# z's projection first, k tile by k tile, z loaded whole per head, and the first W_out weights split during the last merge

## The chip, the cores and the metric

The kernel runs on one core of one Trainium2 chip. The metric is device microseconds from start to end of one execution; lower is better. Engines are called TensorE (PE in the rows, PEld for its weight loads), VectorE (DVE), ScalarE (ACT), GpSimd (POOL) and SyncE (SP, whose queue issues all DMAs here).

## The reference

One layer of a streaming encoder block, 1024 positions of width 1024, all in float32:

```python
h = x @ w_in                                   # 1024 x 7688
(qa, ka, va, ub, qc, kc, vc, zc, bc, ac, gate_a, gate_b, gate_c) = split(h)
ya = chunked_rel_attention(qa, ka, va, rel_bias)          # 8 heads of 64
yb = conformer_conv(ub, ...)                              # GLU, 31 taps, LayerNorm, SiLU
yc = gated_deltanet(qc, kc, vc, zc, bc, ac, ...)          # 4 heads of 128, o * silu(z) at its end
mix = sum over b of sigmoid(gate_b) * (y_b @ w_branch[b])
x = LN1(alpha * x + mix @ w_out)
x = LN2(alpha * x + relu(x @ w_up)**2 @ w_down + sigmoid(x @ w_pg) * (p @ w_pp))
```

`zc` is the 512-column output gate of the third branch: z, used only at the end of `gated_deltanet`.

## The kernel before, in words

Every float32 product is made of three matmuls: each operand is split into a high part (a ScalarE copy to a rounded type) and a low part (the difference, `split_lo`, on VectorE or GpSimd), and high x high, high x low and low x high are summed in a PSUM bank. There are eight banks in three groups, `pj` (2), `fj` (2) and `m` (4) (L93). Most large SBUF tiles are 4 KB slots of one group of 30 (`slot`, L84 to L87), handed out in program order.

The code is a list of steps. A scheduler orders them by priority, which is the order in the program, except that steps inside `tc.high_priority(offset=-1000000)` (L752) come last: they are fillers, which each engine takes up when nothing else is ready. The result is one fixed order of instructions per engine; on SP, too, a DMA that waits holds up all behind it.

- L193 to L203: the transposed x is loaded as two halves of eight k tiles (16 DMAs of 256 KB, first half first), converted and split into `xs` (16 slots).
- `v_proj` (L219), `qk_proj` (L235): the attention's projections. `v_proj` for the first four heads reads weights of 264 columns and writes one `pj` bank per 128 positions. Then 32 steps of attention: `attn_scores` (L257, scores, softmax) and `attn_out` (L284).
- The fillers (L752 to L774): first `side_proj` (L703) for the four 128-column tiles of z, each 48 matmuls into the `fj` banks, copied out by ScalarE (L707) and stored to `z_d` in DRAM; then `side_glu` (L710) for four tiles of the convolution's input, 96 matmuls each (sigmoid tile, then the other), then the 24 tiles of the merge gates. The Conformer convolution (`b_conv`, L634, 30 multiply-adds on VectorE per tile and half, into `ca`) can run as soon as the first GLU tile is in DRAM, its LayerNorm (`b_norm`) behind it.
- DeltaNet: for each head `dn_proj` (L394), `dn_s1` (L419), the 32x32 block inverses (`dn_inv`, L509, 31 dependent pairs of VectorE operations on `X`), `dn_s2` (L532), `dn_scan` (L588, eight dependent steps), `dn_out` (L615). The loop at L795 to L799 starts head h+1's projection before head h's scan. `dn_out` loads z a half at a time into a tile `z` with one buffer (L622), takes Silu, multiplies and stores yc (L631).
- `merge` (L720) three times, for ya, yb and yc: `yload` loads a branch's output back (L689), converts and splits it; each of eight output tiles d is 24 matmuls in `pj` and `fj` banks; sigmoid of the stored gates, product and sum into `mix`. The last merge splits `mix[d]` into `mh`, `ml` (L738, L739).
- Then the pools of that part are closed. `out_cols` (L852) takes 256 columns of W_out at a time: four loads of 256 KB with `lload` (L826), ScalarE copies (L822) and GpSimd splits, then 24 matmuls of 256 columns for each of eight position tiles in an `m` bank. The per-layer input, up and down stages follow; the change does not touch them.

Of the kernel before, what the change touches and what calls it, by code (L numbers as in the profile page):

```python
# [9 lines left out]
F32 = mybir.dt.float32  # L10
F32R = mybir.dt.float32r
# [43 lines left out]
def hybrid_block(ctx, tc, x, xT, pT, w_in, relb, conv_w, conv_b, cln_g, cln_b, dnw, a_log, dt_bias,  # L55
# [10 lines left out]
    def phase(name, waits="pool"):  # L66

        if scoped[0] is not None:
            scoped[0].close()
        st = ExitStack()  # L70
        pool = st.enter_context(tc.tile_pool(name=name, bufs=1, reuse_waits=waits))
        scoped[0] = st

        def alloc(shape, dt, tag, bufs, name):
            return pool.tile(shape, dt, tag=tag, bufs=bufs, name=name)

        return alloc
# [8 lines left out]
    def slot(shape, dt=F32, name="g"):  # L86
        return gp.tile(shape, dt, tag="g", bufs=NSLOT, name=name)  # L87
# [27 lines left out]
    def split_lo(eng, lo, src, hi):  # L115
        eng.tensor_tensor(lo, src, hi.bitcast(F32), ALU.subtract)  # L116
# [23 lines left out]
    def wview(w, k0, kt, c0, cols):  # L140
        return w[k0 * P:(k0 + kt) * P, c0:c0 + cols].rearrange("(k p) c -> p k c", p=P)
# [49 lines left out]


    xs = [(slot([P, T], F32R, name=f"xh{k}"), slot([P, T], F32R, name=f"xl{k}")) for k in range(NK)]  # L193
    xr = []
    for hf in range(2):
        sl = slice(512 * hf, 512 * hf + 512)
        for k in range(NK):
            if hf == 0:
                xr.append(slot([P, T], name="xr"))
            raw = xr[k][:, sl]  # L200
            SY.dma_start(raw, xT[k * P:(k + 1) * P, sl])
            S.activation(xs[k][0][:, sl], raw, AF.Copy)
            split_lo(V, xs[k][1][:, sl], raw, xs[k][0][:, sl])  # L203

    ya_d = dr.tile([4, P, T], F32, name="ya_d")
    yb_d = dr.tile([4, P, T], F32, name="yb_d")
# [2 lines left out]
    gc_d = dr.tile([CH * NT, P], F32, name="gc_d")  # L209
    glu_d = dr.tile([4, P, T], F32, name="glu_d")  # L210
    cv_d = dr.tile([4, P, T], F32, name="cv_d")
    z_d = dr.tile([4, P, T], F32, name="z_d")
    sg_d = dr.tile([3, NK, P, T], F32, name="sg_d")


# [316 lines left out]
    def dn_s2(h, o):  # L532
# [52 lines left out]
        for hf in hfs:  # L585
            V.tensor_copy(ch3(o["W"])[:, hf * 4:hf * 4 + 4, :], pw[hf])

    def dn_scan(h, o):  # L588
        O = o["vb"]
        ss = mp.tile([P, 8], F32, tag="ss", bufs=4, name="ss")  # L590
        st = None
        for c in range(NT):
            cs = slice(c * P, (c + 1) * P)
            pb = bank("m", name="scan")
            pb2 = bank("m", name="scano")
            pk, pss, po = pb[:, 0:P], pb[:, P:2 * P], pb2[:, 0:P]
            vn = O[:, cs]
            if c > 0:
                PE.matmul(pk, lhsT=o["W"][:, cs], rhs=st, start=True, stop=True)
                V.tensor_tensor(vn, vn, pk, ALU.subtract)  # L600
                PE.matmul(po, lhsT=o["qg"][:, cs], rhs=st, start=True, stop=False)
            if c < NT - 1:
                PE.matmul(pss, lhsT=o["kdec"][:, cs], rhs=vn, start=True, stop=True)
                ns = mp.tile([P, P], F32, tag="S", bufs=2, name="S")
                if c == 0:
                    V.tensor_copy(ns, pss)
                else:
                    V.scalar_tensor_tensor(ns, st, vec["egl"][:, h, c:c + 1], pss, ALU.mult, ALU.add)
                st = ns
            PE.matmul(po, lhsT=o["aT"][:, cs], rhs=vn, start=(c == 0), stop=True)  # L610
            S.activation(vn, po, AF.Copy, scale=o["rq"][:, c:c + 1])
            S.activation(po, po, AF.Square, scale=o["rq"][:, c:c + 1], accum_out=ss[:, c:c + 1])
        return O, ss

    def dn_out(h, O, ss):  # L615
        V.tensor_scalar(ss, ss, 1.0 / P, RMS_EPS, ALU.mult, ALU.add)
        r = mp.tile([P, 8], F32, tag="ss", bufs=4, name="r")
        pow_mh(r, ss, 8)
        for hf in range(2):
            sl = slice(512 * hf, 512 * hf + 512)  # L620
            c8 = slice(4 * hf, 4 * hf + 4)
            z = dn([P, 512], F32, "z", 1, "z")  # L622
            SY.dma_start(z, z_d[h][:, sl])
            S.activation(z, z, AF.Silu)
            V.tensor_tensor(ch3(O)[:, c8, :], ch3(O)[:, c8, :], bc_last(r[:, c8], P), ALU.mult)
            tp = bank("m", name="to")
            for c4 in range(4):
                c = hf * 4 + c4
                PE.transpose(tp[:, c4 * P:(c4 + 1) * P], O[:, c * P:(c + 1) * P], ident)
            V.scalar_tensor_tensor(O[:, sl], tp, ng_s[:, 0:1], z, ALU.mult, ALU.mult)  # L630
            SY.dma_start(yc_d[h][:, sl], O[:, sl])  # L631
# [71 lines left out]
    def side_proj(off, func, dst, name):  # L703

        for _, sl, r in side_mm(off, name):
            t = fs([P, 512], F32, "fs", 3, "fs")
            S.activation(t, r, func)  # L707
            SY.dma_start(dst[:, sl], t)

    def side_glu(i):  # L710
# [5 lines left out]
        for h, sl, r in side_mm(O_UB + P * i, f"fa{i}"):  # L716
            V.tensor_tensor(sg[h], r, sg[h], ALU.mult)
            SY.dma_start(glu_d[i][:, sl], sg[h])

    def merge(b, dram, first, last):  # L720
        ys = yload(dram)
        for d in range(NK):
            wb = [wload(wview(w_branch[b], 0, 4, P * d, P), 4, P, f"wbr{b}{d}")]
            if first:
                mix[d] = slot([P, T], name=f"mix{d}")
            for hf, sl, py in mm_b(ys, wb, tag=("pj", "fj"), name="pbr"):
                sg = fs([P, 512], F32, "fs", 3, "sgl")
                SY.dma_start(sg, sg_d[b, d][:, sl])
                S.activation(sg, sg, AF.Sigmoid)
                if first:  # L730
                    V.tensor_tensor(mix[d][:, sl], py, sg, ALU.mult)
                else:
                    V.tensor_tensor(sg, py, sg, ALU.mult)
                    V.tensor_tensor(mix[d][:, sl], mix[d][:, sl], sg, ALU.add)
            if last:
                mh = slot([P, T], F32R, name=f"mh{d}")
                ml = slot([P, T], F32R, name=f"ml{d}")
                S.activation(mh, mix[d], AF.Copy)  # L738
                split_lo(V, ml, mix[d], mh)  # L739
                mixs[d] = (mh, ml)  # L740
# [7 lines left out]
    def cp(shape, dt, tag, bufs, name):  # L748
        return fpool.tile(shape, dt, tag=tag, bufs=bufs, name=name)

    at = phase("at")
    with tc.high_priority(offset=-1000000):  # L752
        for h in range(CH):
            side_proj(O_ZC + P * h, AF.Copy, z_d[h], f"fz{h}")
        adt = cst.tile([P, 8], F32, name="adt")
        SY.dma_start(adt[:, 0:4], rows_bcast(a_log, 4))
        SY.dma_start(adt[:, 4:8], rows_bcast(dt_bias, 4))
        dnw_s = cload(dnw, [P, 12, KC], "dnw_s")
        cw_s = cload(conv_w, [P, 4, KB], "cw_s")
        cb_s = cload(conv_b, [P, 4], "cb_s")  # L760
        cg_s = cload(cln_g, [P, 4], "cg_s")
        cbb_s = cload(cln_b, [P, 4], "cbb_s")
        ng_s = cload(norm_g.rearrange("a (p o) -> p (a o)", o=1), [P, 1], "ng_s")
        for i in range(4):
            side_glu(i)
        for n, (b, d) in enumerate([(b, d) for b in range(3) for d in range(NK)]):
            side_proj(O_GATE[b] + P * d, AF.Copy, sg_d[b, d], f"fg{b}{d}")
            if n in (8, 12):
                for i in range(4):
                    b_conv(i, 0 if n == 8 else 1)  # L770
            if n in range(12, 12 + 4 * 1, 1):
                b_norm((n - 12) // 1)
            if n in range(17, 17 + 4 * 1, 1):
                b_norm(4 + (n - 17) // 1)  # L774
# [11 lines left out]
        return dn_s1(h, dn_proj(h))  # L786

    def dn_b(h, o):
        dn_s2(h, o)
        dn_out(h, *dn_scan(h, o))  # L790

    st = [None] * CH
    st[0] = dn_a(0)
# [32 lines left out]
    def lload(src, kt, cols, name):  # L826
        raw = lraw(name + "r")
        v = raw.rearrange("p (k c) -> p k c", k=kt)
        SY.dma_start(v, src)
        hi, lo = hilo(raw, name, G)  # L830
        return hi.rearrange("p (k c) -> p k c", k=kt), lo.rearrange("p (k c) -> p k c", k=kt)
# [19 lines left out]

    def out_cols(q):  # L852
        c0 = 256 * q
        ws = [lload(wview(w_out, k0, 2, c0, 256), 2, 256, f"wo{q}{k0}") for k0 in range(0, NK, 2)]
        for t in range(NT):
            xr = eo([P, 256], F32, "xres", 4, "xres")
            SY.dma_start(xr, xv[:, t, c0:c0 + 256])
            po = bank("m", name="pout")[:, :256]
            mm_a(Acc(po, 24), mixs, ws, slice(t * P, t * P + P))
            V.scalar_tensor_tensor(x1[t][:, c0:c0 + 256], xr, ALPHA, po, ALU.mult, ALU.add)  # L860
            V.bn_stats(lst[t][:, q, :], x1[t][:, c0:c0 + 256])
            if q == 3:
                ln1_t(t)
# [434 lines left out]
```

## Time and profile before

| | |
|---|---|
| runs | 1966.6, 1966.61, 1970.63 us, median 1966.61 |
| profiled execution | 1967.85 us, of which the span from first to last instruction is 1965.8 |
| instructions | 25832, of them 9265 matmuls |
| TensorE busy | 95% of the span |
| VectorE, ScalarE, GpSimd busy | 64%, 43%, 23% |
| mean granted TensorE clock | 0.979 |
| DMA | 244.66 MB, 124 GB/s on average |

A matmul counts as busy from its start to its modelled end, and consecutive ones overlap, so pitch (start to start) and counts tell more of TensorE than busy time. Idle time of an engine that is not the bottleneck costs nothing. PEclk is the granted TensorE clock as a share of 2.4 GHz.

### The profile page before, as it was taken

What the parts mean: (1) busy time and instruction counts of PE and PEld (TensorE: products, weight loads), DVE (VectorE), ACT (ScalarE), POOL (GpSimd) and SP (SyncE); (2) the same over time, 40 slices, a digit from 0 to 9 for tenths busy, and PEclk for the clock granted to TensorE, in tenths of its full rate; (3) what the DMA queues carried; (4) which work ended last, traced back from release to release, by engine and by line L of the source; (5) the groups of instructions that cost most, each with busy time, mean ns of one, the idle gap of its engine ahead of it and who ended that gap; (6) DMA issues with size and microseconds to landing.
All of it is one profiled execution on the core that took longest, in us unless ns stands there. A gap on an engine that the chain in (4) does not pass through costs nothing. (4 is left out here: it accounts for less than half of the span.)

```text
span 1965.8 us, 25832 instructions
## 1 busy us (share of the span) xinstructions
PE 1858.8 (95%) x9265; PEld 1553.0 (79%) x9265; DVE 1252.4 (64%) x2193; ACT 848.1 (43%) x1534; POOL 460.1 (23%) x385
## 2 busy tenths in 40 slices
PE   7999999999999989999999999989999999999996
PEld 6889887787777868777877898768888877778775
DVE  3343499799997747673376348764433326875978
ACT  4544545553332343433454216545555544333333
POOL 3323323343323122222120233223222310000001
PEclk9999999999999999999999999999999999999998
DMA  6212222133423233243453535763332357652542
GB/s 187 55 52 77 66 65 65 50 92 91 135 67 99 74 91 102 74 136 90 148 186 116 178 109 177 252 209 128 108 119 96 125 218 240 219 167 95 184 145 90
DMA packets 211471, 244.66 MB, mean 124 GB/s; under 512 B 23888, under 2 KB 130448, under 8 KB 211344
## 3 DMA queue, kind: packets, MB, share of 16 engines
q1 hardware_dynamic: 211344, 243.03, 39.0%
q8 instruction: 73, 1.20, 0.3%
q14 instruction: 54, 0.44, 0.1%
HBM read 183.17 MB, written 59.80 MB: 124 GB/s over the span
## 5 line engine op out<-in xcount | busy, mean ns | idle before, releaser
L646 DVE SCALAR_TENSOR_TENSOR ca<-ci,cw_s,ca 128x512 f32<-128x512 f32 x240 | 208.0, 867 | 3.2
L942 PE MATMUL pda<-bh,ah 128*128 128x512 f32 x256 | 97.6, 396 | 8.9 <-ACT bh L1160 7.8
L190 POOL TENSOR_TENSOR mv<-mv,nhalf 128x1 f32<-128x1 f32 x16 | 17.2, 1086 | 362.2 <-DVE mv L653 362.2
L943 PE MATMUL pda<-bl,ah 128*128 128x512 f32 x256 | 100.7, 393 | 0.0
L944 PE MATMUL pda<-bh,al 128*128 128x512 f32 x256 | 100.4, 393 | 0.0
L280 POOL TENSOR_SCALAR st<-st,mx 128x640 f32<-128x640 f32 (+2 forms) x64 | 51.4, 805 | 177.1 <-DVE mx L279 161.8
L942 PE MATMUL pdb<-bh,ah 128*128 128x512 f32 x192 | 74.8, 402 | 7.7 <-DVE x L1202 7.7
L1160 ACT ACTIVATE ah<-draw 128x1024 fp32r<-128x1024 f32 x32 | 33.9, 1060 | 102.8 <-PE pda L943 51.3
L1113 DVE TENSOR_TENSOR r<-puc,r 128x512 f32<-128x512 f32 x16 | 11.1, 692 | 103.3 <-PE puc L944 103.3
L943 PE MATMUL pdb<-bl,ah 128*128 128x512 f32 x192 | 76.4, 398 | 0.0
L944 PE MATMUL pdb<-bh,al 128*128 128x512 f32 x192 | 75.7, 397 | 0.0
L277 ACT ACTIVATE st<-st,mx 128x640 f32<-128x640 f32 (+2 forms) x64 | 44.5, 696 | 69.3 <-DVE mx L273 69.2
L942 PEld LDWEIGHTS pda<-bh,ah 128*128 128x128 f32 x256 | 48.6, 190 | 20.9 <-ACT bh L1160 9.0
L273 DVE CUSTOM_DVE_ANT_0 st<-sc,nb 128x320 f32<-128x320 f32 (+2 forms) x64 | 30.8, 485 | 45.9 <-PE sc L271 42.9
L944 PEld LDWEIGHTS pda<-bh,al 128*128 128x128 f32 x256 | 48.8, 190 | 10.3
L943 PEld LDWEIGHTS pda<-bl,ah 128*128 128x128 f32 x256 | 48.8, 191 | 10.2
L707 ACT ACTIVATE fs<-fj 128x512 f32<-128x512 f32 x56 | 33.0, 589 | 49.0 <-PE fj L164 30.7
L116 DVE TENSOR_TENSOR al<-draw,ah 128x1024 fp32r<-128x1024 f32 x32 | 39.1, 1221 | 23.0 <-ACT ah L1160 23.0
L307 ACT ACTIVATE ph<-tp 128x512 fp32r<-128x512 f32 (+2 forms) x72 | 36.6, 525 | 39.6 <-PE tp L303 31.3
L404 DVE SCALAR_TENSOR_TENSOR c<-pc,dnw_s,c 128x511 f32<-128x511 f32 (+2 forms) x72 | 52.5, 732 | 1.4 <-ACT c L402 1.2
L527 DVE TENSOR_TENSOR X<-X,tm 32x31 f32<-32x31 f32 (+15 forms) x124 | 50.9, 411 | 2.4
L116 DVE TENSOR_TENSOR pl<-tp,ph 128x512 fp32r<-128x512 f32 (+2 forms) x72 | 42.3, 595 | 14.9 <-ACT ph L307 14.3
(1589 smaller groups left out, 6276.5 us busy)
## 6 DMA issues: line engine op xcount, KB each, us to landing
draw<-h_d SPq DMA_DIRECT2D x48, 512.0 KB, 4.8
wu<-in_w_up_dram SPq DMA_DIRECT2D x32, 512.0 KB, 3.9
h_d<-r SPq DMA_DIRECT2D x64, 256.0 KB, 2.2
draw<-in_w_down_dram SPq DMA_DIRECT2D x32, 512.0 KB, 5.1
sg_d<-fs SPq DMA_DIRECT2D x48, 256.0 KB, 2.2
sgl<-sg_d SPq DMA_DIRECT2D x48, 256.0 KB, 3.0
wg<-in_w_pg_dram SPq DMA_DIRECT2D x36, 256.0 KB, 5.5
cb<-in_w_down_dram SPq DMA_DIRECT2D x16, 512.0 KB, 8.5
```

The lines of the kernel that those rows point to most:

```text
L116: eng.tensor_tensor(lo, src, hi.bitcast(F32), ALU.subtract)
L277: S.activation(st[:, :nk], st[:, :nk], AF.Exp, scale=-1.0, bias=mx[:, nm:nm + 1], accum_out=mx[:, 2:3])
L280: G.tensor_scalar(st[:, :nk], st[:, :nk], mx[:, 3:4], 1.0, ALU.mult, ALU.mult)
L307: S.activation(ph[:, :n], tp[:, :n], AF.Copy)
L404: V.scalar_tensor_tensor(acc[:, 512 * hf + s_:512 * hf + 512], pp[:, :512 - s_], cw[:, 3 - s_:4 - s_], acc[:, 512 * hf + s_:512 * hf + 512 ...
L527: V.tensor_tensor(X3[:, jj + 1:32, 0:ncol], X3[:, jj + 1:32, 0:ncol], tv, ALU.subtract)
L646: V.scalar_tensor_tensor(acc, t[:, H - s_:H - s_ + 512], cw_s[:, i, H - s_:KB - s_], acc, ALU.mult, ALU.add)
L707: S.activation(t, r, func)
L942: PE.matmul(out_, lhsT=ah, rhs=bh, start=first, stop=False, skip_group_check=True)
L943: PE.matmul(out_, lhsT=ah, rhs=bl, start=False, stop=False, skip_group_check=True)
L944: PE.matmul(out_, lhsT=al, rhs=bh, start=False, stop=last, skip_group_check=True)
L1160: S.activation(hi, src, AF.Copy)
```

## The change

z is computed before anything else: `z_start` reserves all eight banks (two halves of four tiles), loads x and z's weights k tile by k tile and adds each k tile's 24 matmuls as it arrives. ScalarE then copies the banks out to `z_d`. The splits of z's weights are VectorE's. The four `side_proj` calls for z are gone from the fillers. Before a head's `dn_s2`, `z_load` loads the whole z of the head into a slot and takes Silu once; `dn_out` reads halves of it. In the last merge, before `mix[4]` is split, `wo_first` loads the first 256 columns of W_out into slots, in two loads of 512 KB, and splits them on ScalarE and VectorE; `out_cols(0)` uses these.

```diff
-    xr = []
-    for hf in range(2):
-        sl = slice(512 * hf, 512 * hf + 512)
+    z_d = dr.tile([4, P, T], F32, name="z_d")
+
+    def z_start():
+        banks = {}
+        for i, tag in enumerate(("m", "m", "pj", "fj")):
+            for h in range(2):
+                banks[i, h] = bank(tag, name="pz")
+
+        def zmm(i, h, lhsT, rhs, first, last):
+            PE.matmul(banks[i, h], lhsT=lhsT, rhs=rhs, start=first, stop=last, skip_group_check=True)
+
         for k in range(NK):
-            if hf == 0:
-                xr.append(slot([P, T], name="xr"))
-            raw = xr[k][:, sl]
-            SY.dma_start(raw, xT[k * P:(k + 1) * P, sl])
-            S.activation(xs[k][0][:, sl], raw, AF.Copy)
-            split_lo(V, xs[k][1][:, sl], raw, xs[k][0][:, sl])
+            raw = slot([P, T], name="xr")
+            xh, xl = xs[k]
+            for h in range(2):
+                sl = slice(h * 512, h * 512 + 512)
+                SY.dma_start(raw[:, sl], xT[k * P:(k + 1) * P, sl])
+                if h == 0:
+                    wr = wp.tile([P, 528], F32, tag="wr", bufs=2, name=f"wz{k}r")[:, :512]
+                    SY.dma_start(wr, w_in[k * P:(k + 1) * P, O_ZC:O_ZC + 512])
+            wh = wp.tile([P, 528], F32R, tag="wh", bufs=6, name=f"wz{k}h")[:, :512]
+            wl = wp.tile([P, 528], F32R, tag="wl", bufs=6, name=f"wz{k}l")[:, :512]
+            S.activation(xh[:, 0:512], raw[:, 0:512], AF.Copy)
+            S.activation(wh, wr, AF.Copy)
+            split_lo(V, xl[:, 0:512], raw[:, 0:512], xh[:, 0:512])
+            split_lo(V, wl, wr, wh)
+            S.activation(xh[:, 512:], raw[:, 512:], AF.Copy)
+            split_lo(V, xl[:, 512:], raw[:, 512:], xh[:, 512:])
+            for h in range(2):
+                sl = slice(h * 512, h * 512 + 512)
+                for n, (w, xx) in enumerate(((wh, xh), (wh, xl), (wl, xh))):
+                    for i in range(4):
+                        zmm(i, h, w[:, i * P:(i + 1) * P], xx[:, sl], k == 0 and n == 0, k == NK - 1 and n == 2)
+        for h in range(2):
+            for i in range(4):
+                t = fs([P, 512], F32, "fs", 3, "fs")
+                S.activation(t, banks[i, h], AF.Copy)
+                SY.dma_start(z_d[i][:, h * 512:h * 512 + 512], t)
...
+    def z_load(h, o):
+        z = o["z"] = slot([P, T], name=f"z{h}")
+        SY.dma_start(z, z_d[h])
+        S.activation(z, z, AF.Silu)
+
...
-    def dn_out(h, O, ss):
+    def dn_out(h, o, O, ss):
...
-            z = dn([P, 512], F32, "z", 1, "z")
-            SY.dma_start(z, z_d[h][:, sl])
-            S.activation(z, z, AF.Silu)
+            z = o["z"][:, sl]
...
+    def wo_first():
+
+        for kk in range(2):
+            raw = slot([P, 4, 256], name=f"wo{kk}r")
+            hi, lo = slot([P, 4, 256], F32R, name=f"wo{kk}h"), slot([P, 4, 256], F32R, name=f"wo{kk}l")
+            SY.dma_start(raw, wview(w_out, 4 * kk, 4, 0, 256))
+            S.activation(hi, raw, AF.Copy)
+            split_lo(V, lo, raw, hi)
+            wo0.extend((hi[:, 2 * i:2 * i + 2, :], lo[:, 2 * i:2 * i + 2, :]) for i in range(2))
+
...
+            if last and d == 4:
+                wo_first()
             if last:
                 mh = slot([P, T], F32R, name=f"mh{d}")
...
+    z_start()
     at = phase("at")
     with tc.high_priority(offset=-1000000):
-        for h in range(CH):
-            side_proj(O_ZC + P * h, AF.Copy, z_d[h], f"fz{h}")
...
     def dn_b(h, o):
+        z_load(h, o)
         dn_s2(h, o)
-        dn_out(h, *dn_scan(h, o))
+        dn_out(h, o, *dn_scan(h, o))
...
-        ws = [lload(wview(w_out, k0, 2, c0, 256), 2, 256, f"wo{q}{k0}") for k0 in range(0, NK, 2)]
+        ws = wo0 if q == 0 else [lload(wview(w_out, k0, 2, c0, 256), 2, 256, f"wo{q}{k0}") for k0 in range(0, NK, 2)]
```

## Rows read from the trace of the kernel before

**Rows 1.** The page's busy time, share of the span and instructions of each engine.

```profile
PE 1858.8 (95%) x9265; PEld 1553.0 (79%) x9265; DVE 1252.4 (64%) x2193; ACT 848.1 (43%) x1534; POOL 460.1 (23%) x385
```

**Rows 2.** Stretches: length, busy us (count) of PE, PEld, DVE, ACT, POOL; PEclk, DMA share, GB/s.

```profile
0.00:57.00 57.00, 44.78 (x251) 38.86 (x252) 20.10 (x34) 22.14 (x40) 18.59 (x25) 0.97 0.53 162
83.00:236.50 153.50, 153.50 (x895) 135.02 (x895) 63.28 (x184) 78.18 (x163) 49.01 (x59) 1.00 0.23 64
236.50:502.00 265.50, 255.49 (x1293) 212.77 (x1292) 237.70 (x445) 131.90 (x265) 91.13 (x81) 0.98 0.26 74
502.00:631.00 129.00, 118.85 (x529) 95.81 (x528) 115.99 (x227) 39.15 (x86) 43.64 (x26) 0.96 0.35 97
1043.30:1060.00 16.70, 13.26 (x45) 10.01 (x45) 8.02 (x12) 6.76 (x9) 1.45 (x2) 0.80 0.26 93
1086.00:1100.00 14.00, 9.22 (x52) 8.60 (x51) 4.07 (x6) 4.40 (x7) 7.98 (x6) 0.76 0.79 250
1750.00:1800.00 50.00, 50.00 (x222) 41.39 (x222) 29.58 (x30) 19.57 (x20) 0.00 (x0) 1.00 0.25 81
```

**Rows 3.** The same for tiles pv, fj and pv alone: columns PE, PEld, DVE, ACT.

```profile
0.00:57.00 57.00, 29.20 (x192) 27.39 (x192) 3.39 (x14) 2.61 (x8) 0.97 0.53 162
...
0.00:57.00 57.00, 19.90 (x59) 12.62 (x60) 0.00 (x0) 1.19 (x2) 0.97 0.53 162
...
50.90:56.90 6.00, 6.00 (x48) 5.81 (x47) 0.50 (x2) 0.38 (x1) 1.00 0.00 0
```

**Rows 4.** Timeline of the start: start, us, engine, operation, count, idle before and releaser.

```profile
3.59 0.63 ACT L202 ACTIVATE xh<-xr 128x512 fp32r<-128x512 f32 x1 [1.51 <-DMA xr<-in_xT_dram]
...
4.61 0.63 ACT L202 ACTIVATE xh<-xr 128x512 fp32r<-128x512 f32 x1 [0.40 <-DMA xr<-in_xT_dram]
...
6.61 0.81 PE L164 MATMUL pv<-wv00h,xh 128*128 128x264 f32 x2 [6.61 <-ACT wv00h L133]
...
14.06 0.63 PE L164 MATMUL fj<-xl,fz0h 128*128 128x512 f32 x1
...
14.49 0.63 PE L164 MATMUL fj<-xh,fz0l 128*128 128x512 f32 x1
...
82.82 0.80 PE L269 MATMUL sc<-kh,q 128*128 128x128 f32 x4
```

**Rows 5.** The same for fj (PE, PEld, DVE, ACT), ca (DVE, ACT), X (DVE, POOL).

```profile
83.00:236.50 153.50, 54.56 (x220) 40.48 (x221) 0.68 (x1) 4.18 (x7) 1.00 0.23 64
...
236.50:370.00 133.50, 80.48 (x92) 0.00 (x0) 0.97 0.23 63
...
510.00:625.00 115.00, 27.01 (x63) 1.74 (x1) 0.96 0.35 98
...
864.00:899.00 35.00, 21.89 (x63) 1.26 (x1) 0.95 0.29 85
```

**Rows 6.** Timeline around the last head's output and the last merge's start.

```profile
1038.41 0.46 SPq L631 DMA_DIRECT2D yc_d<-c  x1
...
1043.38 0.32 SPq L689 DMA_DIRECT2D yr<-yc_d  x1
...
1045.92 0.75 DVE L630 SCALAR_TENSOR_TENSOR c<-to,ng_s,z 128x512 f32<-128x512 f32 x1 [9.18 <-ACT z L624]
...
1046.70 0.32 SPq L631 DMA_DIRECT2D yc_d<-c  x1
...
1046.90 0.79 PE L164 MATMUL pbr<-yh,wbr20h 128*128 128x512 f32 x1 [3.44 <-ACT yh L690]
...
1048.71 0.32 SPq L689 DMA_DIRECT2D yr<-yc_d  x1
```

**Rows 7.** Timeline around the first W_out matmul.

```profile
1089.82 1.23 DVE L116 TENSOR_TENSOR ml<-mix,mh 128x1024 fp32r<-128x1024 f32 x1 [1.18 <-ACT mh L738]
...
1090.36 1.12 PE L164 MATMUL pout<-wo00h,mh 128*128 128x256 f32 x4 [4.03 <-ACT wo00h L822]
```

**Rows 8.** Timeline of TensorE in the down stage.

```profile
1703.12 1.07 PE L942 MATMUL pda<-bh,ah 128*128 128x512 f32 x4
```

More of the change, by code (lines that the diff above doesn't have):

```diff
@@ L211, in hybrid_block @@
     cv_d = dr.tile([4, P, T], F32, name="cv_d")
-    z_d = dr.tile([4, P, T], F32, name="z_d")
     sg_d = dr.tile([3, NK, P, T], F32, name="sg_d")
@@ L718, in side_glu @@
             SY.dma_start(glu_d[i][:, sl], sg[h])
+    wo0 = []
+    def wo_first():
[6 more added lines that the diff above has]
+            wo0.extend((hi[:, 2 * i:2 * i + 2, :], lo[:, 2 * i:2 * i + 2, :]) for i in range(2))
     def merge(b, dram, first, last):
```

## Prediction

> **What bounds the kernel now.** The page comes first: TensorE is busy for 95% of the span and no other engine for more than 64% [rows 1], so time goes only where TensorE stands or runs at half clock. The table by stretches says where that is [rows 2]. Full speed is taken from the down stage: 222 matmuls of 512 columns in 50.0 us at clock 1.00, a pitch of 0.225 us. A 264-column one takes 6.00 / 48 = 0.125 us [rows 3]; a 256-column one I put at half of 0.225, 0.113 us. Three of the stretches are what the change aims at:
> - 0 to 57 us holds 192 matmuls of v_proj and 59 fillers of z [rows 3]: 192 x 0.125 + 59 x 0.225 = 37.3 us of work, so 19.7 us are lost. The first matmul starts at 6.61 us, and at 14 us two matmuls still stand 0.43 us apart, the 1.2 GHz level [rows 4].
> - 1043.3 to 1060 us holds 45 matmuls, 10.1 us of work: 6.6 us lost, 3.4 of them in one wait for the last head of yc [rows 6], the rest at half clock behind it (0.80 over 16.7 us is 6.7 us at half).
> - 1086 to 1100 us holds 52 matmuls, nearly all of W_out: 5.9 us of work, 8.1 lost. TensorE waits 4.03 us for the first W_out weights [rows 7] and then runs some 6.7 us at half clock (0.76 of 14).
>
> From 83 to 236.5 us TensorE is never idle. From 236.5 to 631 VectorE is the full engine, 90% busy in both stretches [rows 2]. TensorE's instructions stand in one fixed order, so a stretch of it without waits can't get shorter by moving work within it; only a loss can go.
>
> **Start.** z's 192 matmuls are not new: they leave the filler queue and come first. The second transfer of the program is converted at 4.61 us [rows 4]; in the changed order that place is held by z's first weights, so the first matmul can go at 4.61 + 0.63 = 5.2 us. Each k tile brings three transfers of 256 KB. At the 162 GB/s that the first 57 us average [rows 2] the 786 KB take 4.9 us; ScalarE needs 3 x 0.63 us, VectorE three splits of 512 columns, where one of 1024 takes 1.23 [rows 7]. The 24 matmuls of a k tile take 5.4 us at full clock and 10.3 at half, so loads and conversions lie under them; without that cover the eight k tiles would go at the feed's pace, 8 x 4.9 = 39 us, which is still less than the 43.2 of the matmuls. The weight loads wait for one of two raw buffers, and behind each on SP stands the next x load; with 5.4 us of matmuls per turn that wait is covered too. The clock: from the two later stretches I take 6.7 us at half, which loses 3.3; upper end 9.3 us (5.2 to the slow pair at 14.5 [rows 4]), 4.6 lost. Handing the banks over: the third of eight ScalarE copies frees v_proj's first bank, 1.9 us, while half 1 still has 12 matmuls, 2.7 us. Between nothing and 8 x 0.63 = 5.0 us I take 1.0, close to the cover. Loss 5.2 + 3.3 + 1.0 = 9.5 us against 19.7: **10.2 us won** (5.5 to 11.2). The eight low-half splits move from GpSimd to VectorE, which is 35% busy there: nothing.
>
> Here a rule speaks against the change. The row: four matmuls to four different banks take 1.07 us in the down stage [rows 8], and that stretch holds clock 1.00 [rows 2]. The Trainium skill, TensorE: Matmul & The Clock Gate (A second HAM failure mode: psum-queue depth-cycling), says that moving through the banks every iteration can make TensorE idle in small pieces until its clock swings between the two levels. The trace does not show that where the banks alternate. By that rule z's 192 matmuls would stay at half clock and the start's gain would become a loss; it is the fourth rival below.
>
> **The main chain is delayed, and VectorE gives it back.** What the start wins is only free if the chain attention, DeltaNet heads, yc, merge 2 isn't late, since TensorE already waits at its end for the last head [rows 6]. Attention's first score matmul starts at 82.8 us [rows 4]. After the change it can start at 5.2 + 3.3 + 43.2 (z) + 1.0 + 24.0 (v_proj) + 21.6 (96 matmuls of q and k) = 98.3: **15.5 us later**. Against that, the fillers no longer begin with z. They run at 220 in 153.5 us beside attention [rows 5], and the Conformer convolution, which starts at 236.5 us, needs 72 of them (the sigmoid tile and half a GLU tile). So it can start near 98 + 50 = 150 us, in a stretch where VectorE is now only 41% busy [rows 2]. VectorE has 63.3 + 237.7 + 116.0 = 417.0 us of work between 83 and 631. Filled from 150 on, with three lulls of about 23 us (96 filler matmuls take 67 us, 30 taps of convolution 92 in 133.5, 44 us [rows 5]) and 10% idle otherwise: 98 + 52 (21 us of work) + 69 (35) + 361 / 0.9 (401) = 620 us instead of 631. The first head's inverse shows the mechanism: its 63 VectorE instructions need the stretch 510 to 625 with the convolution between them and 864 to 899 without it [rows 5]. So I take the chain as **10 us early**. Its ends: 15.5 us late (nothing recovered) and 28 us early (no lulls).
>
> **z in one slot.** For the last head the second z half can't be loaded until the first has been used: VectorE stands 9.18 us for it, and the second yc store is issued 8.3 us after the first [rows 6]. With z there early both stores follow each other. The first half's reload comes 5.0 us after its store with that load between them on SP, the second's 2.0 us after its own [rows 6]; I take 3.0 us off the first. The four Silu of 1024 columns replace eight of 512 and lie under TensorE. The price is a slot: 16 of x, 5 for each of two heads, 3 of the next projection and this one make 30 of 30, so the next head's k copy can wait for the scan, with SP's z load and the loads behind it. No row has that wait; below it is nothing, above I set the longest wait for z now, 9.2 us [rows 6], for three heads. I take nothing, as that head's chain goes on only when the scan ends anyway, and keep the upper end inside the 15.5 us above.
>
> Sum at merge 2: other work is done at 1043.3 - 10.2 = 1033.1, the last head is there at 1046.9 - 3.0 - 10 = 1033.9. TensorE goes on at 1033.9 without cooling, where before it went on at 1046.9 and lost 3.0 more: **16.0 us**.
>
> **W_out.** Two loads of 512 KB, two ScalarE copies and two VectorE splits (about 1.1 and 1.2 us each, as the split of mix [rows 7]) go into the last merge, where TensorE is never idle; the four loads, four copies and four GpSimd splits after it go. Next in line is the last mix tile, whose low half is ready at 1091.05 [rows 7], 4.7 us after the merge's last matmul; seven k tiles of four output tiles, 84 x 0.113 = 9.5 us, can run before it. I leave 1.0 of the 8.1 us: **7.1 us** (4 to 8).
>
> **Sum.** 16.0 + 7.1 = 23.1 us off the profiled execution's 1967.85 gives 1944.7; that execution lies 1.2 above the median of the runs, so 1943.5, given as 1944. TensorE's 20 us of waits between 236.5 and 631 [rows 2] fall anew with any new order; I let them move by 6 either way.
>
> **Rivals.**
> 1. *The chain stays late (slower).* If VectorE gives nothing back, the last head comes at 1046.9 - 3.0 + 15.5 = 1059.4, TensorE waits and cools (3.0): 12.5 us lost against 7.1 won, **1972**. It decides from a chain 10.1 us late on: as late as now 3.0 + 7.1 are won, and each us more takes one. For it: TensorE already waits for this chain. Against: the half-empty VectorE before 236.5. Chance 0.13.
> 2. *Half recovered.* The chain is as late as now, the start's gain is mostly waited away: 3.0 + 7.1, **1956.5**. Chance 0.20.
> 3. *W_out's weights don't come early*: no slot is free in the merge, or the load stands on SP behind gate loads; 16.0 remain, **1950.6**. This is where the change wouldn't do what it says. Chance 0.10.
> 4. *Bank after bank keeps the clock low*: 192 x (0.43 - 0.225) less the 3.3 counted, 36 us more at the start, on both sides of merge 2: **1980**. Against it stand [rows 8]. Chance 0.02.
>
> **Numbers.** The forecast has 0.53, and 0.02 is left for what I don't see, counted slower. About 0.2% is what a measurement of this kernel can tell from no change. Faster: 0.53 + 0.10 + 0.15 of rival 2 = 0.78. Within 0.2%: the rest of 2 and 0.03 of 1, 0.08. Slower: 0.14. The range: below, all lulls gone (1.0), the start at its best (1.0), W_out wholly gone (1.0) and 6 of other waits and some 2 of spread, 1932; above it takes in rivals 2 and 3 with 6 of other waits and the lower ends of the start and of W_out, 1966. That leaves out rivals 1 and 4 and little else.
>
> **What the profile of the changed kernel would show.** Right: first matmul near 5 us, 0.225 us between z's matmuls from about 12 us, first score near 98, convolution from about 150, the inverse of head 0 in clearly less than 115 us, no wait over 1 us for yh before merge 2, the first W_out matmul straight behind the last merge matmul. Wrong: a wait for yh of over 4 us at merge 2 (rival 1 or 2), pauses at each k tile in the first 50 us (feed), or new TensorE waits of over 10 us between 236 and 1033.

## The result and the profile after

The kernel after takes 1944.63 us (median of 4 runs, 1942.02 to 1946.67) against 1967.22 for the kernel before beside it: ratio 0.9888, interval [0.9861, 0.9914]. Its profiled execution took 1944.56 us, with a span of 1942.8. In a second set of runs, beside the last experiments, the same kernel gave 1949.31 against 1963.3: ratio 0.9930 [0.9915, 0.9945]. So the gain is 14 to 22 us by the ratios, and the two intervals do not overlap. Both sets are faster by over 0.2% and inside the range; the forecast of 1944 was met by the first set alone.

The page's busy time of after, beside [rows 1]: TensorE is busy for 8.7 us less, VectorE does what it did.

```profile
PE 1850.1 (95%) x9265; PEld 1543.4 (79%) x9265; DVE 1258.3 (65%) x2203; ACT 831.1 (43%) x1516; POOL 445.0 (23%) x373
```

The stretches of after with the columns of [rows 2], and one more from the start's middle:

```profile
0.00:57.00 57.00, 51.78 (x227) 42.46 (x228) 19.35 (x30) 25.86 (x43) 13.91 (x21) 1.00 0.68 211
...
9.50:51.00 41.50, 41.50 (x180) 33.67 (x179) 15.88 (x21) 18.57 (x32) 10.42 (x10) 1.00 0.64 191
...
83.00:236.50 153.50, 153.50 (x867) 133.26 (x866) 112.55 (x247) 77.21 (x155) 58.12 (x55) 1.00 0.24 68
236.50:502.00 265.50, 256.08 (x1292) 211.34 (x1291) 224.01 (x426) 126.98 (x266) 96.89 (x86) 0.99 0.26 75
...
1086.00:1100.00 14.00, 14.00 (x122) 14.00 (x121) 5.37 (x11) 1.06 (x1) 0.00 (x0) 1.00 0.38 124
```

From 9.5 to 51 us TensorE never stands: 180 matmuls in 41.5 us, a pitch of 0.231 us, and all of them go bank after bank. VectorE's work between 83 and 236.5 has nearly doubled, from 63.3 [rows 2] to 112.6 us: the convolution has moved there. Between 1086 and 1100, where 8.1 us were lost, nothing is. The same view for two tiles, the convolution's ca (DVE, ACT) and head 0's inverse X (DVE, POOL):

```profile
83.00:236.50 153.50, 54.42 (x62) 0.00 (x0) 1.00 0.24 68
...
569.00:610.00 41.00, 27.69 (x63) 1.25 (x1) 0.96 0.21 58
```

62 of the convolution's instructions run there, 54.4 us of them, and the 63 of the inverse now lie in 41 us. The stretch of 115 us in [rows 5] was longer than the inverse itself. In before 62 of its 63 instructions lie in these 86 us (columns DVE, POOL):

```profile
536.00:622.00 86.00, 26.92 (x62) 0.89 (x1) 0.96 0.26 72
```

So the inverse takes about half the time it took.

The timeline of the start (columns of [rows 4]), then the first score matmul, the convolution's first instruction and head 0's px:

```profile
4.53 0.63 ACT L217 ACTIVATE wz0h<-wz0r 128x512 fp32r<-128x512 f32 x1
...
5.21 2.07 PE L203 MATMUL pz<-xh,wz0h 128*128 128x512 f32 x4 [5.21 <-ACT wz0h L217]
...
7.08 1.91 PE L203 MATMUL pz<-xl,wz0h 128*128 128x512 f32 x4
...
8.79 1.35 PE L203 MATMUL pz<-xh,wz0h 128*128 128x512 f32 x4
...
9.98 1.09 PE L203 MATMUL pz<-xh,wz0l 128*128 128x512 f32 x4
10.90 1.10 PE L203 MATMUL pz<-xl,wz0h 128*128 128x512 f32 x4
...
108.17 0.39 PE L296 MATMUL sc<-kh,q 128*128 128x128 f32 x2
...
152.04 0.55 DVE L674 TENSOR_SCALAR ca<-ci,cw_s,cb_s 128x512 f32<-128x512 f32 x1 [0.92 <-DMA ci<-glu_d]
...
620.46 1.95 PE L578 MATMUL px<-T,LT 128*128 128x128 f32 x16
```

The first four matmuls start 1.87 us before the next four (0.47 us each on average, twice the later pitch, so the 1.2 GHz level); the group at 9.98 us takes 0.92 (0.23 each, the 2.4 GHz level). The granted clock can be read only from 9.35 us on, where its records in this trace begin, with 1.00; the 1.00 of the row from 0 to 57 says nothing of the time before that.

The timeline around merge 2, where [rows 6 and 7] showed the waits, and W_out:

```profile
1019.05 1.40 DVE L660 SCALAR_TENSOR_TENSOR c<-to,ng_s,z 128x512 f32<-128x512 f32 x2
...
1020.07 0.93 SPq L661 DMA_DIRECT2D yc_d<-c  x2
...
1024.36 0.32 SPq L719 DMA_DIRECT2D yr<-yc_d  x1
...
1026.53 0.39 PE L164 MATMUL pbr<-yh,wbr17l 128*128 128x512 f32 x1
1026.76 0.39 PE L164 MATMUL pbr<-yh,wbr20h 128*128 128x512 f32 x1
...
1071.71 0.39 PE L164 MATMUL pbr<-yh,wbr27l 128*128 128x512 f32 x1
...
1071.94 0.28 PE L164 MATMUL pout<-wo0h,mh 128*128 128x256 f32 x1
```

Both halves of the last head leave together, wbr20 (merge 2's first weights) follows wbr17 without a gap, and the first W_out matmul comes 0.23 us behind the last one of the merge, 18.4 us earlier than in [rows 7].

**Where the time came from.** For every kernel TensorE's loss in a stretch is counted in one way: its length less its matmuls at the median pitch of their shape in the trace of before (512 columns 0.230 us, 264 0.1215, 256 0.117, 128 0.110). From before to after: 0 to 57 us 20.1 to 7.4; 300 to 650 35.0 to 33.2; 650 to 1000 **32.1 to 38.3**; 1000 to 1060 7.2 to 1.2. Together with 0.3 more lost from 57 to 300 these give 14.0 us, and the last merge matmul indeed starts 14.3 us earlier. W_out's stage, from there to the last pout matmul, adds 9.7 (8.4 lost, now nothing). The stages behind it take 1.0 us more.

### The profile page after: what moved, and what is told of

It is laid out like the page before. It is cut to its first block, busy times and chain, and to the rows that moved or that the text cites. A ratio compares the mean times of both kernels' runs of the same rounds, so it can differ in the third digit from the quotient of the medians.

```text
span 1942.8 us, 25812 instructions
## 1 busy us (share of the span) xinstructions
PE 1850.1 (95%) x9265; PEld 1543.4 (79%) x9265; DVE 1258.3 (65%) x2203; ACT 831.1 (43%) x1516; POOL 445.0 (23%) x373
## 5 line engine op out<-in xcount | busy, mean ns | idle before, releaser
L676 DVE SCALAR_TENSOR_TENSOR ca<-ci,cw_s,ca 128x512 f32<-128x512 f32 x240 | 214.2, 892 | 3.8
L190 POOL TENSOR_TENSOR mv<-mv,nhalf 128x1 f32<-128x1 f32 x16 | 17.4, 1094 | 360.9 <-DVE mv L683 360.9
L307 POOL TENSOR_SCALAR st<-st,mx 128x640 f32<-128x640 f32 (+2 forms) x64 | 58.7, 919 | 179.8 <-DVE mx L306 174.2
L987 PEld LDWEIGHTS pda<-bl,ah 128*128 128x128 f32 x256 | 48.7, 190 | 10.2 <-DVE bl L116 0.2
L553 DVE TENSOR_TENSOR tm<-X 32x31 f32<-32x31 f32 (+15 forms) x124 | 53.4, 431 | 3.0
L771 ACT ACTIVATE sgl<-sgl 128x512 f32<-128x512 f32 x48 | 30.2, 631 | 50.0 <-DMA sgl<-sg_d 41.5
L116 POOL TENSOR_TENSOR wu2l<-wu,wu2h 128x512 fp32r<-128x512 f32 x16 | 20.8, 1303 | 128.1 <-ACT wu2h L866 128.1
```

What stands on the lines that cost most here:

```text
L307: G.tensor_scalar(st[:, :nk], st[:, :nk], mx[:, 3:4], 1.0, ALU.mult, ALU.mult)
L553: V.tensor_tensor(tv, bc_last(L, ncol), bc_mid(R, nr), ALU.mult)
L676: V.scalar_tensor_tensor(acc, t[:, H - s_:H - s_ + 512], cw_s[:, i, H - s_:KB - s_], acc, ALU.mult, ALU.add)
L987: PE.matmul(out_, lhsT=ah, rhs=bl, start=False, stop=False, skip_group_check=True)
```

## Experiments

All compute the whole result. The first table tells where each one's chain stood (us from the start of the span; the last column is TensorE's wait), the second TensorE's losses in us.

| kernel | ratio to before [interval] | convolution from | last head's `to` ends | wait for yh at merge 2 |
|---|---|---|---|---|
| before | 1 | 234.8 | 1035.5 | 3.4 |
| after, first and second set | 0.9888 [0.9861, 0.9914], 0.9930 [0.9915, 0.9945] | 152.0 | 1018.3 | 0 |
| zfirst_alone | 0.9923 [0.9905, 0.9942] | 151.9 | 1020.1 | 2.3 |
| zslot_alone | 0.9983 [0.9970, 0.9996] | 233.9 | 1028.8 | 0 |
| wout_alone | 0.9968 [0.9949, 0.9986] | 234.0 | 1034.7 | 3.4 |
| no_zslot | 0.9908 [0.9891, 0.9924] | 152.3 | 1023.9 | 2.1 |
| no_wout | 0.9922 [0.9903, 0.9942] | 152.2 | 1021.0 | 0 |
| conv_later | 0.9975 [0.9955, 0.9995] | 267.9 | 1046.2 | 5.9 |
| z_behind_glu | 0.9940 [0.9918, 0.9962] | 86.2 | 981.6 | 0 |
| z_first_by_tile | 0.9968 [0.9953, 0.9984] | 180.8 | 999.7 | 0 |
| zbg_wout | 0.9924 [0.9911, 0.9937] | 86.2 | 978.8 | 0 |
| glu_first | 0.9848 [0.9832, 0.9865] | 54.6 | 1005.0 | 0 |
| glu_first_noslot | 0.9899 [0.9882, 0.9917] | 53.9 | 985.0 | 0 |

| TensorE's loss | 0 to 57 | 300 to 650 | 650 to 1000 | 1000 to 1060 | 1060 to 1120 |
|---|---|---|---|---|---|
| before | 20.1 | 35.0 | 32.1 | 7.2 | 8.5 |
| after (first profile) | 7.4 | 33.2 | 38.3 | 1.2 | 0 |
| zfirst_alone | 7.4 | 32.9 | 31.4 | 5.1 | 7.6 |
| no_zslot | 7.9 | 33.8 | 33.7 | 5.1 | 0.1 |
| conv_later | 6.9 | 45.6 | 31.7 | 14.3 | 0.8 |
| z_behind_glu | 23.2 | 17.4 | 41.3 | 0.7 | 6.4 |
| z_first_by_tile | 19.4 | 34.4 | 30.9 | 1.1 | 5.9 |
| glu_first | 7.5 | 18.5 | 30.7 | 1.1 | 0 |
| glu_first_noslot | 7.0 | 19.7 | 36.7 | 0.7 | 0 |

**The parts alone.** The theory is that of the prediction: three gains, of which the start's reaches merge 2 only because the convolution, started earlier, takes VectorE's work forward. Each of the first three kernels is before with one part of the change.

zfirst_alone (`z_start` in place of the old loads of x, and z's lines out of the filler queue):

```
+    z_start()
     at = phase("at")
...
-        for h in range(CH):
-            side_proj(O_ZC + P * h, AF.Copy, z_d[h], f"fz{h}")
```

> The kernel before with the start alone (z first in eight banks); z still loaded by halves in the head's end, W_out's first weights still late. Theory (the start's 12.8 us are won and the chain recovers its delay through the earlier convolution, without help from the z slot): no wait over 2 us for yh at merge 2, the last merge ends 13 to 17 us earlier than in the kernel before, the 4 us wait for W_out and the cool stretch behind it stay: 1951 us (1948 to 1955). Rival (the z slot is what brings the chain forward): a wait for yh of over 4 us stays at merge 2 and most of the start's gain is waited away: 1957 to 1966 us.

Measured: 0.9923, 15 us at before's median of 1964. The loss at the start is that of after, the chain ends 15.4 us earlier than in before, without help from the slot, and one short wait is left at merge 2; the first row is W_out's, as in [rows 7]:

```profile
PE pout L164 <- ACT wo00h L848: 4.4, 1, 4.4
PE pbr L164 <- ACT yh L717: 2.3, 1, 2.3
```

The yh wait is 0.3 over what was expected and far from the rival's 4. The last merge matmul starts 17.5 us earlier than in before, just over the 13 to 17 expected. The theory holds.

zslot_alone (only `z_load` and its use):

```
     def dn_b(h, o):
+        z_load(h, o)
...
-            z = dn([P, 512], F32, "z", 1, "z")
-            SY.dma_start(z, z_d[h][:, sl])
-            S.activation(z, z, AF.Silu)
+            z = o["z"][:, sl]
```

> The kernel before with z per head in one slot alone. Theory: both halves of the last head are stored together, the second one some 8 us earlier; the wait for yh at merge 2 (3.44 us) and the half clock behind it (3 us) go nearly wholly, nothing else moves: 1961 us (1960 to 1964). Rival (the thirtieth slot delays the next head's k copy): a wait for that slot shows in the heads and the time is that of the kernel before or up to 5 us over it: 1967 to 1972 us.

Measured: 0.9983, 3.3 us. The wait for yh is gone and the loss between 1000 and 1060 falls from 7.2 to 1.0, as expected. But between 650 and 1000 the loss rises from 32.1 to 38.4, which takes all of that back; what is left is 3.1 us of other waits between 300 and 650. That is the first sign of the slot's price; the wait for a slot, which the rival had, does not show.

wout_alone (only `wo_first` and its use):

```
+            if last and d == 4:
+                wo_first()
...
+        ws = wo0 if q == 0 else [...]
```

> The kernel before with the first W_out weights split during the last merge alone. Theory: the first W_out matmul follows straight behind the last merge matmul, the 8.1 us lost between 1086 and 1100 us go to about 1; the wait for yh at merge 2 stays at about 3.4 us: 1960 us (1958 to 1962). Rival (no slot is free in the last merge, or the load stands behind gate loads on SP): the wait in front of W_out stays over 2 us: 1964 to 1967 us.

Measured: 0.9968, 6.3 us: a slot is free in the merge, no wait for W_out's weights is left, and the loss from 1060 to 1120 goes from 8.5 to 2.1. The profiled execution took 1965.4 us, against a median of 1958.4: its last pout matmul ends 10.7 us earlier than in before, but 8.2 of these are gone again at the end, lost in stages that the edit leaves alone. So the trace shows what the part does, and its worth to the end is known only as the ratio's interval has it, 3 to 10 us. The three parts add to 24.7 us by ratios, the whole gave 14 to 22.

**After without one part.** no_zslot puts the three old lines for z back:

> The kernel after with z loaded by halves in the head's end again, as in the kernel before. Theory (with the chain 9 us ahead of merge 2 the slot buys nothing that TensorE sees): the second half of the last head's yc is stored some 8 us later than the first, the wait for yh at merge 2 stays under 3 us: 1945 us (1942 to 1949). Rival (the slot is part of the gain at merge 2): a wait for yh of over 4 us and the cooling behind it come back: 1950 to 1954 us.

Measured: 0.9908, between the two sets of after: whether the slot buys anything there can't be told. The stretches of after and then of no_zslot (columns of [rows 2]) show why:

```profile
850.00:900.00 50.00, 42.04 (x192) 34.26 (x193) 33.42 (x91) 15.72 (x41) 10.02 (x9) 0.90 0.29 82
...
1000.00:1060.00 60.00, 59.77 (x265) 48.27 (x264) 44.58 (x59) 26.16 (x44) 12.31 (x9) 1.00 0.49 163
```

```profile
850.00:900.00 50.00, 46.65 (x235) 38.64 (x234) 33.30 (x91) 16.68 (x42) 10.44 (x9) 0.97 0.30 85
...
1000.00:1060.00 60.00, 57.80 (x250) 46.04 (x249) 38.25 (x53) 25.13 (x41) 10.96 (x8) 0.97 0.43 141
```

With the slot TensorE issues 15 matmuls more between 1000 and 1060 (the yh wait is gone) and 43 fewer between 850 and 900. There the third head's scan runs, in small matmuls that wait for VectorE, while VectorE also inverts the fourth head's triangles. In after fewer other matmuls stand in TensorE's written order beside that scan. Between its first and last matmul there are 173 of fillers and merges in zslot_alone, after and no_wout, which have the slot, and 218 in before, zfirst_alone, wout_alone and no_zslot, which don't. Between these two matmuls TensorE loses 15.5 to 17.6 us in the first three and 4.0 to 6.6 in the other four. The waits in after:

```profile
PE scan L635 <- DVE c L632: 3.9, 2, 3.6
PE scan L631 <- DVE S L640: 2.1, 1, 2.1
```

In no_zslot the same two are 1.6 and 0.4 us. The granted clock of the stretch falls with them, from 0.97 to 0.90. The slot wins 3.9 us between 1000 and 1060 (5.1 to 1.2), and 4.6 were lost before that, from 650 to 1000 (33.7 to 38.3).

no_wout takes `wo_first` out of after:

> The kernel after without the early W_out weights. Theory (this part stands by itself, whatever the chain does): a 4 us wait for wo00h comes back behind the last merge matmul, and the half clock behind it; 7 us over the kernel after (5 to 9), ratio to the kernel before 0.9915 to 0.9935. Rival (behind an undisturbed merge 2 the weights would be there anyway): no wait over 1.5 us in front of W_out, ratio 0.989.

Measured: 0.9922, inside the band expected. The waits in front of W_out are back, as its rows show, and its stretch 1060 to 1120 loses 6.5 us:

```profile
PE pout L164 <- ACT wo00h L852: 3.2, 1, 3.2
PE pout L164 <- POOL wo00l L116: 0.9, 1, 0.9
```

The times by themselves don't separate it from after's second set; the waits do.

**Is it the convolution?** conv_later is after with four gate tiles of branch 0 ahead of the GLU tiles:

```
+        for d in range(4):
+            side_proj(O_GATE[0] + P * d, AF.Copy, sg_d[0, d], f"fg0{d}")
         for i in range(4):
             side_glu(i)
```

> The kernel after with four gate tiles (192 filler matmuls) put ahead of the four GLU tiles, so that the Conformer convolution starts late again; the start, the z slot and W_out's early weights stay. Theory (the start's gain reaches merge 2 only because the earlier convolution pulls VectorE's work forward): convolution from about 260 us instead of 152.6, head 0's px over 630 us instead of 620.5, a wait for yh of 8 to 25 us at merge 2; 10 to 25 us over the kernel after, ratio to the kernel before 0.994 to 1.002. Rival (the order of the fillers is indifferent, VectorE has slack elsewhere): head 0's px stays near 620 us, no wait over 3 us for yh, the time of the kernel after, ratio 0.989.

Measured: 0.9975; some 9 to 17 us of the change's gain are gone. The convolution starts at 267.9 us, head 0's px at 656, and merge 2 waits for the last head twice, at its scan's end and for yh:

```profile
1044.27 1.97 PE L659 MATMUL to<-ident,c 128*128 128x128 f32 x8 [3.45 <-DVE c L655]
...
1052.17 0.79 PE L164 MATMUL pbr<-yh,wbr20h 128*128 128x512 f32 x1 [5.93 <-ACT yh L720]
```

The wait for yh is shorter than the 8 expected; both together are 9.4, and the loss around them 14.3. The rival falls: this is the mechanism of the prediction's rival 1 made to happen. The start's 13 us are won and then waited away, 10.6 of them between 300 and 650 us, and the last merge matmul starts 4.2 us later than in before. W_out's gain stays, so the kernel is not slower, as rival 1 had it.

z_behind_glu is before with z's four lines moved behind the loop over `side_glu`, and nothing else:

> The kernel before with z's four filler tiles moved behind the four GLU tiles, and nothing else. Theory (the place of z in the filler queue is what delays the convolution and with it the chain): convolution from about 130 us instead of 236.5, the chain 10 to 30 us earlier, the wait for yh at merge 2 and the half clock behind it gone, the loss at the start (20.0 us) and at W_out as they were: 4 to 7 us under the kernel before, ratio 0.9965 to 0.998. Rival (the chain is bound by the heads' own order, not by the convolution): the wait for yh stays, ratio 1.000.

Measured: 0.9940, 11.8 us, about twice what was expected. The convolution starts at 86.2 us, not at 130, the chain ends 54 us earlier, not 10 to 30, and beside merge 2's gap TensorE's waits between 300 and 650 us halve. This stretch in before, then in z_behind_glu:

```profile
300.00:650.00 350.00, 329.89 (x1618) 272.05 (x1617) 304.11 (x582) 143.68 (x301) 117.75 (x90) 0.97 0.31 88
```

```profile
300.00:650.00 350.00, 339.10 (x1735) 282.94 (x1735) 287.14 (x624) 148.48 (x321) 110.38 (x93) 1.00 0.29 83
```

TensorE issues 117 matmuls more in the same time, at clock 1.00 instead of 0.97; VectorE, which it waits for there, is busy for 17 us less. Of the 17.6 us won there 9.2 are lost again between 650 and 1000. Moving these lines alone wins 11.8 us, where the whole change wins 14 to 22, and it wins them elsewhere: nothing at the start, and most between 300 and 650 us, where after is hardly better than before.

**Are eight banks needed?** z_first_by_tile puts `side_proj` of z's four tiles ahead of attention at normal priority, in its two banks, with x loaded as before:

> The kernel before with z's tiles put first on TensorE but tile by tile in their two banks, with x still loaded by halves and split as before; no z slot, no early W_out. Theory (eight banks, k tile by k tile, are what lets TensorE work at the pace at which x lands): TensorE loses 12 to 20 us up to 57 us instead of 7.2, since a tile needs all eight k tiles of a half before it ends; the chain recovers as with the start alone; ratio 0.995 to 0.999, against 0.9923 of the start alone. Rival (mere priority is enough, the second half of x comes in time): loss of 7 to 9 us, ratio 0.992 to 0.994.

Measured: 0.9968. TensorE loses 19.4 us up to 57, as much as before, standing 6.1 us for x beside the 6.5 at the very start:

```profile
PE fj L164 <- ACT fz0h L133: 6.5, 1, 6.5
PE fj L164 <- ACT xh L202: 5.3, 5, 2.2
PE fj L164 <- DVE xl L116: 0.8, 3, 0.5
```

So mere priority wins nothing at the start. What wins is z_start as a whole: eight banks, k tile by k tile, with x and z's weights loaded in that order and split on VectorE; no run takes these apart. What this kernel still gains is merge 2: convolution from 180.8, no wait for yh. The Trainium skill, TensorE: Matmul & The Clock Gate (HAM oscillation — how this bites in real kernels), advises for a thin M to do all k tiles of one M tile before waiting for a DMA. Here x itself is still landing, and the order tile by tile loses 19.4 us, the one k tile by k tile 7.4.

**Versions built on this.** zbg_wout joins z_behind_glu and wout_alone, without the new start or the slot:

> The kernel before with z's tiles moved behind the GLU tiles and W_out's first weights early, without the new start and without the z slot. Theory (the parts add up): 0.9940 and 0.9968 give 0.9908, some 18 us under the kernel before, although TensorE still loses 20 us or more up to 57 us. Rival (both parts fill the same hole around the last merge): 0.993 to 0.995.

Measured: 0.9924 [0.9911, 0.9937], as fast as after beside it (0.9930), though it still loses 23 us at the start. The two parts alone would give 0.9908, which lies outside the interval, and the rival's 0.993 lies inside it: some 3 us are missing, and that the parts add up is not shown.

glu_first is after with two GLU tiles in the eight banks, and z's tiles behind the other two:

```
-                    SY.dma_start(wr, w_in[k * P:(k + 1) * P, O_ZC:O_ZC + 512])
+                    wv = w_in[k * P:(k + 1) * P, O_UB:O_UB + 2 * MIX].rearrange("p (a c) -> p a c", a=2)
+                    SY.dma_start(wr.rearrange("p (a c) -> p a c", a=2), wv[:, :, 0:2 * P])
...
-        for i in range(4):
+        for i in range(2, 4):
             side_glu(i)
+        for h in range(CH):
+            side_proj(O_ZC + P * h, AF.Copy, z_d[h], f"fz{h}")
```

> The kernel after with the first two GLU tiles (sigmoid and value columns) in the eight banks at the start in place of z; z's four tiles go into the filler queue behind the other two GLU tiles. Theory (an earlier convolution is worth something of its own: it takes VectorE's work out of the stretch where TensorE waits for VectorE between 300 and 650 us, as in the kernel with z behind the GLU tiles, where TensorE lost 17.7 us there against 32.1 in the kernel after): convolution from about 58 us instead of 152.6, TensorE's loss up to 57 us as in the kernel after (7 us), its loss from 300 to 650 about 18 us, 5 to 8 given back later; 5 to 10 us under the kernel after, ratio to the kernel before 0.983 to 0.987. Rival (with merge 2 no longer waiting, an earlier chain buys nothing): the waits of 300 to 650 us only move behind 650; ratio 0.988 to 0.990.

Measured: 1933.65 us, 0.9848 [0.9832, 0.9865]; **it beats both kernels**, after by some 16 us in the same set. The convolution's first instruction and the stretch of 300 to 650:

```profile
54.57 0.55 DVE L676 TENSOR_SCALAR ca<-ci,cw_s,cb_s 128x512 f32<-128x512 f32 x1 [0.55 <-DMA ci<-glu_d]
...
300.00:650.00 350.00, 339.22 (x1755) 281.58 (x1754) 238.24 (x542) 152.24 (x336) 106.12 (x100) 1.00 0.29 83
```

Against after's first profile it loses 8.8 us more between 57 and 300 (11.6 for 2.7), 14.7 less from 300 to 650 and 7.6 less from 650 to 1000. The rival (nothing to win once merge 2 doesn't wait) falls.

> The same kernel (two GLU tiles first) with z loaded by halves in the head's end. Theory (the slot moves TensorE's loss from merge 2 to the third head's scan, and with a chain 40 us early merge 2 needs nothing): TensorE's loss between 850 and 900 us 5 to 7 us smaller, no wait for yh over 1 us at merge 2; 0 to 6 us under the same kernel with the slot. Rival (the slot is a gain wherever heads end): 3 to 6 us over it.

Measured: 0.9899 [0.9882, 0.9917], 10 us slower than with the slot by the ratios and 8.6 by the profiled spans (1938.1 and 1929.5): the expectation was wrong, and the rival's figure too low. No single wait carries it: without the slot the loss is 6.0 us higher from 650 to 1000, 1.2 higher from 300 to 650, and merge 2 waits in neither. So the slot is worth 3 us alone, about 10 here, and in after an amount that two sets of runs leave between 4 lost and 4 won. What it does is change the order in which TensorE's instructions stand, and here it does so the other way: beside the third head's scan stand 175 filler and merge matmuls with the slot and 126 without, and TensorE loses 11.2 and 15.0 us there. Why the scheduler's order comes out better in one case than in another stays open.

> The kernel after once more, beside the three above: the ratio seen first was 0.9888 [0.9861, 0.9914], so 0.987 to 0.991; each part alone gave 0.9923 (start), 0.9983 (z slot) and 0.9968 (W_out), together 0.9875.

Measured: 0.9930, outside what was expected. In the stretches of the table its losses are those of the first profile within 2.1 us (650 to 1000: 40.4 against 38.3), so the mechanism is the same; after's median is 4.7 us higher in this set and before's 3.9 lower. What makes the sets differ isn't known.

## Why the prediction was right

The direction and the mechanisms held: the start's gain, a chain that recovers through the earlier convolution, and W_out's weights on time. That the time came within 1 us in the first set is partly luck. Three terms of the sum were off and largely cancelled, and the second set, with nearly the same losses, gave 4.7 us more.

- **Start**: 10.2 us forecast, 12.7 won (11.4 at the prediction's own pitches), over the upper end of 11.2. The lower end of 5.5 does not follow from the terms given, which make 4.9 (19.7 less 5.2, 4.6 and 5.0). The first matmul came at 5.21, as forecast. Half clock lasted only until about 9.4 us, so it cost 2.1 instead of 3.3, and handing over the banks cost nothing: v_proj's first matmul starts at 51.7 us, straight behind z's last at 51.5. The loads and conversions stayed under the matmuls.
- **Delay of the chain**: 15.5 us forecast, 25.4 measured (first score 108.2). The step that failed is v_proj's 24.0 us: between 51.7 and 108.2 us the filler queue, which now begins with GLU, puts 44 matmuls of 512 columns, 10.1 us, between those of v_proj, q and k. I had counted the fillers out of that stretch. The same fillers give it back: the convolution needs 72 of them, and the 72nd starts at 143.3 us, where the forecast had 148.
- **Recovery**: forecast 25.5 us (15.5 late to 10 early), measured 35.9 (25.4 late to 10.5 early): px of head 0 at 620.5, forecast 620, in spite of the later start; the last head is 17.2 early. The convolution started at 152.0 (forecast 150), and head 0's inverse takes about 40 us. I had read 115 us for it in before; it was 86. conv_later shows that the early convolution is what carries the recovery.
- **z slot**: forecast 3.0 us at merge 2 and no cost. Alone it is worth 3.3, in after nothing that can be told: the slot's price was looked for in a wait for a slot, and it came as fewer filler matmuls beside the third head's scan, which loses 15.5 us for before's 5.9. From 650 to 1000 us 6.2 us more were lost, a price that the sum had put at nothing.
- **Merge 2**: 16.0 forecast, 14.3 measured. The losses make 14.0 of it: 12.7 of the start, 6.0 of the gap and 1.8 of other waits, less 6.2 and 0.3.
- **W_out**: 7.1 forecast (4 to 8), 9.7 by the pout stage of the two profiles, 6.3 by wout_alone's ratio. The last mix tile, feared as next in line, was ready: nothing is lost behind the merge.
- **Rivals**: 1 needs the late convolution (conv_later) and didn't happen; 2 neither; 3 neither, as wout_alone shows; 4 fell with the row of 9.5 to 51 us: pitch 0.231 us and clock 1.00 with eight banks in turn. The rule of the Trainium skill that stood behind rival 4 (TensorE: Matmul & The Clock Gate, A second HAM failure mode: psum-queue depth-cycling) tells of a kernel whose TensorE idles for short times between groups of matmuls as it goes through the banks, and whose clock then swings. Here it went through the banks without idling, so the trace shows that the banks alone don't do it, and does not test the rest. The prediction had priced the worst case, half clock for all of z's matmuls.

What the prediction did not see is that the chain's earliness is worth something beyond merge 2. I left TensorE's waits between 236.5 and 631 out of the sum, with 6 us either way; in after they are nearly so (35.0 to 33.2), but in z_behind_glu and glu_first, whose convolution starts 66 and 97 us earlier still, they halve. glu_first shows it best: its first score comes when after's does (107.4 and 108.2 us), and its convolution 97 us earlier.

## What to carry to other kernels

Look at what stands first in the low-priority queue: work whose result is wanted late (z) in front of work that feeds a long chain on another engine (GLU, then the convolution) cost 12 us here, about as much as the new start won. When operands still land, spreading the first output tiles over all free banks and going k tile by k tile is worth trying, with tiles that unlock the other engines. An edit that changes only a buffer can change the written order of a statically ordered engine (here 173 matmuls instead of 218 beside one scan), so price it in a trace of the whole, not in the place it was made for.

## What the runs showed of the hardware

The half clock at the start of the program lasted from 5.2 to 9.4 us in after, where TensorE never stood (pitch 0.43 from the second matmul on, then 0.23). In before, where it stood for 0.6 us before 8.0 and for 2.0 before 12.6, the pitch stayed at 0.43 until 18.6 us. In both traces the records of the granted clock begin where the pitch falls, so the clock column's 1.00 ahead of that is no reading. In 9.5 to 51 us the pitch of 512-column matmuls was 0.231 us, against 0.225 in the down stage [rows 2], at the same granted clock of 1.00. And two sets of runs of the same two kernels gave ratios 0.4% apart, with intervals that do not overlap.
